# Narrow weight parts start up to 31 columns further into their tiles

## The chip, the cores and the metric

The kernel runs on one core of a Trainium2 chip. The metric is the device time of one execution in microseconds (us). TensorE multiplies, VectorE (DVE), ScalarE (ACT) and GpSimd (POOL) work on elements, and SyncE (SP) issues the transfers from HBM to the on-chip memory (SBUF, 128 partitions).

## The reference

Two transformer blocks, one after the other, on one sequence of 256 tokens with 1024 features, in fp32. The first block mixes gated MLP heads, forgetting attention and attention over a memory, and has a feed-forward layer of 4096. The second has two layers, each of them feed-forward, attention, feed-forward; its four feed-forwards are gated ones with a width of 2816:

```python
def swiglu(h, wg, wu, wd):
    return (jax.nn.silu(h @ wg) * (h @ wu)) @ wd
...
        x = x + 0.5 * swiglu(rmsnorm_2(x, ffn_norm1[i]), ffn1_wg[i], ffn1_wu[i], ffn1_wd[i])
```

Most of the work is the products of 256 tokens with weight matrices, 208.71 MB of which are read once.

## The kernel before

Activations lie transposed in SBUF: a tile holds 128 features (partitions) by 256 tokens. To keep fp32 accuracy with TensorE's fp32r format, each activation and each weight is split in two fp32r numbers, a high and a low part, and each product is made of three matmuls: high by high, low by high, high by low.

The class `Stream` brings in the weights. A list `order`, made from `seq` and `cuts`, names every transfer (a chunk of up to 2048 columns by 128 partitions) and how it is cut into parts of at most `PART = 1024` columns. There are 436 parts, numbered `i` in the order in which they are used. `split()` handles one part: ScalarE copies it from `raw` into the tile `wh{i % 6}` (line 103), which rounds it to fp32r, and one call later `low()` lets VectorE subtract that from `raw` and write the rest to `wl{i % 6}` (line 113). All of these tiles are 1024 columns wide whatever the part's width, and a part begins at column 0 of its tile. `get()` runs this up to `AHEAD = 4` parts ahead of the products. The order on each engine is the order of the program; nothing is reordered by a planner.

`mm_t` (lines 130 to 137) makes the products in which a slice of 128 columns of the weight tile is the stationary operand (loaded by an LDWEIGHTS that the trace calls PEld) and the activation tile of 256 columns is the moving one; each step over `k` has the three matmuls of lines 135, 136 and 137. In `mm_n` (lines 139 to 147) and `mm_y` (lines 149 to 161) the weights are the moving operand.

The parts of at most 768 columns: the down-projections `dn0` to `dn3` of the four gated feed-forwards (each of 16 transfers of 1408 columns, cut into 768 and 640, so 32 parts a stage and 128 in all), four parts of 768 of `w1v`, six parts of 512 or 768 of `uqv0` and `uqv1`, and one of 256 of `bin1`: 139 of 436. The parts of `w1f` have 780 columns. A down-projection loops over 8 output tiles `d`, each with four parts and 6 + 5 + 6 + 5 = 22 steps over `k`:

```python
            for d in range(KT):
                p = bank()
                for k0, n in ((0, DN_CUT), (DN_CUT, 11 - DN_CUT), (11, DN_CUT), (11 + DN_CUT, 11 - DN_CUT)):
                    mm_t(p[:, :T], ws.get(), 0, P, (ah[k0:], al[k0:]), range(n), k0 == 0, k0 == 11 + DN_CUT)
```

So a stage `dn` has 8 x 22 x 3 = 528 pairs of a weight load and a matmul. By the order of the parts, `dn0` has the parts 139 to 170, `dn1` 233 to 264, `dn2` 309 to 340 and `dn3` 404 to 435.

Of the kernel before, what the change touches and what calls it, by code (L numbers as in the profile page):

```python
# [24 lines left out]
PART = 1024  # L25
# [26 lines left out]
def block_kernel(ctx: ExitStack, tc: tile.TileContext, a: dict, out: bass.AP, upto: int = 99):  # L52
# [20 lines left out]
    class Stream:  # L73
# [20 lines left out]
        def split(self, eng=dve):  # L94
            i = self.ns
            while len(self.parts) <= i and self.nd < len(order):
                self.dma()
            if i >= len(self.parts):
                return False
            t, n, last = self.parts[i]  # L100
            h = wp.tile([P, PART], F32R, tag=f"wh{i % HL}", name=f"wh{i}")
            lo = wp.tile([P, PART], F32R, tag=f"wl{i % HL}", name=f"wl{i}")
            act.copy(h[:, :n], t)  # L103
            self.hl[i] = (h, lo)
            self.ns += 1
            self.low(eng)
            self.late = (lo[:, :n], t, h[:, :n], last)
            return True
# [495 lines left out]
    for nm, i0, i1 in seq:  # L604
        for i in range(i0, i1):
            src = [a[nm][i, 0], a[nm][i, 1]] if len(a[nm].shape) == 4 else [a[nm][i]]
            for ap in src:
                n = ap.shape[-1]
# [906 lines left out]
```

## Time and profile before

| | |
|---|---|
| median of 3 runs | 1241.44 us (1239.43 to 1244.65) |
| the profiled execution | 1249.46 us, its span 1247.7 us |
| TensorE, busy share of the span | 98% (9844 matmuls, 9844 weight loads) |
| VectorE, ScalarE, GpSimd, busy share | 67%, 53%, 14% |
| granted TensorE clock, mean | 0.991 |
| HBM read | 208.71 MB, 168 GB/s over the span |

A span runs from the first to the last instruction of the profiled execution. Matmuls overlap, so that a busy TensorE need not be at its peak: its pace is read from the distance between the starts of successive matmuls, here called a step. [...]

### The profile page before, as it was taken

Reading aid. Unit: us, or ns where it says so; the run is one execution under the profiler, and the core shown is the slowest. Engines: PE = TensorE matmul, PEld = TensorE weight load, DVE = VectorE, ACT = ScalarE, POOL = GpSimd, SP = SyncE. Lnnn points to the kernel's source line nnn. Section 1 sums busy time; section 2 is a strip of 40 time slices with the busy share of each in tenths; the row PEclk is TensorE's granted clock in tenths of the full one; section 3 lists DMA queues with packets and bytes.
Section 4 is the critical chain, followed back from the end, with each engine's and each line's share of the span. In section 5 each row is a group of like instructions: output and inputs, shape, how many; then the busy total and the mean of one; then the engine's idle time right before and its main releaser. Section 6 shows DMA issues by size and latency. Waiting matters only on the chain.

```text
span 1247.7 us, 23873 instructions
## 1 busy us (share of the span) xinstructions
PE 1221.4 (98%) x9844; PEld 1165.4 (93%) x9844; DVE 840.4 (67%) x1482; ACT 658.1 (53%) x1164; POOL 175.6 (14%) x169
## 2 busy tenths in 40 slices
PE   8999999999999999999999999999999989999998
PEld 7878899888899999988999999999999869999998
DVE  6786776754578666698666666666666797666553
ACT  5455765443554544577545444445454787545442
POOL 5422200300202001122100001100001462000000
PEclk9799999999999999999999999999999999999999
DMA  7524354655344545532555456545556422555463
GB/s 237 199 89 148 137 199 173 213 196 200 122 152 165 202 144 187 211 136 94 177 185 188 168 166 207 199 173 203 172 168 209 167 68 89 182 184 189 161 203 111
DMA packets 37262, 211.31 MB, mean 169 GB/s; under 512 B 4768, under 2 KB 8224, under 8 KB 18848
## 3 DMA queue, kind: packets, MB, share of 16 engines
q1 hardware_dynamic: 37152, 209.78, 48.6%
q8 instruction: 77, 1.26, 0.4%
q14 instruction: 33, 0.27, 0.1%
HBM read 208.71 MB, written 1.05 MB: 168 GB/s over the span
## 4 chain that ended last, share of the span: by engine, by line
PE 84%; DVE 10%; ACT 3%; issue 2%; DMA 1%; POOL 0%; SPq 0%; ACTq 0%; DVEq 0%
PE ps L135 23%; PE ps L137 23%; PE ps L136 23%; DVE wl L113 3%; PE ps L159 3%; PE ps L161 3%; PE ps L160 3%; PE ps L310 1%; PE ps L342 1%; PE ps L321 1%; DVE p L299 1%; DMA raw<-in_w1q 1%; PE ps L145 1%; PE ps L146 1%; ACT wh L103 1%
## 5 line engine op out<-in xcount | busy, mean ns | idle before, releaser
L113 DVE TENSOR_TENSOR wl<-raw,wh 128x1024 fp32r<-128x1024 f32 (+4 forms) x436 | 491.2, 1165 | 57.1 <-ACT wh L103 56.7
L135 PE MATMUL ps<-xh,wh 128*128 128x256 f32 (+1 forms) x1848 | 522.8, 283 | 2.2 <-DVE y L526 1.7
L137 PE MATMUL ps<-xh,wl 128*128 128x256 f32 (+1 forms) x1848 | 517.6, 280 | 2.5 <-DVE wl L113 2.5
L136 PE MATMUL ps<-xl,wh 128*128 128x256 f32 (+1 forms) x1848 | 518.5, 281 | 0.5 <-DVE xl L271 0.5
L103 ACT CAST wh<-raw 128x1024 fp32r<-128x1024 f32 (+4 forms) x436 | 400.2, 958 | 92.8 <-PE ps L160 37.8
L135 PEld LDWEIGHTS ps<-xh,wh 128*128 128x128 f32 (+1 forms) x1848 | 348.9, 189 | 5.0 <-ACT sq L208 2.1
L137 PEld LDWEIGHTS ps<-xh,wl 128*128 128x128 f32 (+1 forms) x1848 | 348.9, 189 | 3.0 <-DVE wl L113 2.9
L136 PEld LDWEIGHTS ps<-xl,wh 128*128 128x128 f32 (+1 forms) x1848 | 348.9, 189 | 0.9 <-DVE xl L271 0.7
L137 PE MATMUL ps<-ah,wl 128*128 128x256 f32 x704 | 195.7, 278 | 0.0
L136 PE MATMUL ps<-al,wh 128*128 128x256 f32 x704 | 195.4, 278 | 0.0
L135 PE MATMUL ps<-ah,wh 128*128 128x256 f32 x704 | 195.4, 278 | 0.0
L408 ACT ACTIVATE s<-t 128x256 f32<-128x256 f32 x88 | 36.9, 419 | 189.1 <-DVE t L406 189.1
L136 PEld LDWEIGHTS ps<-al,wh 128*128 128x128 f32 x704 | 132.3, 188 | 0.0
L137 PEld LDWEIGHTS ps<-ah,wl 128*128 128x128 f32 x704 | 132.2, 188 | 0.0
L135 PEld LDWEIGHTS ps<-ah,wh 128*128 128x128 f32 x704 | 131.9, 187 | 0.0
L209 POOL TENSOR_TENSOR acc<-acc,sq 128x256 f32<-128x256 f32 x49 | 55.2, 1127 | 516.7 <-ACT sq L208 516.2
L406 DVE TENSOR_TENSOR t<-ps,rb 128x256 f32<-128x256 f32 x88 | 37.2, 422 | 71.6 <-PE ps L137 65.0
L262 ACT ACTIVATE xh<-x,cols 128x256 fp32r<-128x256 f32 x56 | 28.5, 509 | 105.9 <-DVE x L454 94.6
L223 DVE TENSOR_TENSOR al<-f,ah 128x256 fp32r<-128x256 f32 (+1 forms) x104 | 48.8, 470 | 52.5 <-ACT ah L222 52.5
L222 ACT CAST ah<-f 128x256 fp32r<-128x256 f32 (+1 forms) x104 | 45.7, 440 | 56.6 <-DVE f L410 43.2
L410 DVE TENSOR_TENSOR f<-ps,s 128x256 f32<-128x256 f32 x88 | 37.4, 425 | 47.5 <-ACT s L408 47.5
L453 DVE SCALAR_TENSOR_TENSOR t<-ps,rb 128x256 f32<-128x256 f32 x32 | 13.6, 425 | 74.0 <-PE ps L137 74.0
(278 smaller groups left out, 1422.2 us busy)
## 6 DMA issues: line engine op xcount, KB each, us to landing
raw<-in_gu SPq DMA_DIRECT2D x88, 1024.0 KB, 4.8
raw<-in_dn SPq DMA_DIRECT2D x64, 704.0 KB, 4.4
raw<-in_ff SPq DMA_DIRECT2D x32, 1024.0 KB, 4.8
raw<-in_w_out SPq DMA_DIRECT2D x4, 1024.0 KB, 4.8
raw<-in_aq SPq DMA_DIRECT2D x4, 1024.0 KB, 5.0
raw<-in_a_out SPq DMA_DIRECT2D x4, 1024.0 KB, 5.7
raw<-in_b_out SPq DMA_DIRECT2D x4, 1024.0 KB, 5.0
raw<-in_w1q SPq DMA_DIRECT2D x6, 512.0 KB, 4.1
```

The lines of the kernel that those rows point to most:

```text
L103: act.copy(h[:, :n], t)
L113: eng.tensor_tensor(out=lo, in0=t, in1=h.bitcast(F32), op=ALU.subtract)
L135: pe.matmul(ps, lhsT=h[:, c:c + m], rhs=x[0][k], start=s0, stop=False)
L136: pe.matmul(ps, lhsT=h[:, c:c + m], rhs=x[1][k], start=False, stop=False)
L137: pe.matmul(ps, lhsT=lo[:, c:c + m], rhs=x[0][k], start=False, stop=s1)
L159: pe.matmul(ps, lhsT=x[0][k][:, ts], rhs=h[:, c:c + n], start=s0, stop=False)
L160: pe.matmul(ps, lhsT=x[1][k][:, ts], rhs=h[:, c:c + n], start=False, stop=False)
L161: pe.matmul(ps, lhsT=x[0][k][:, ts], rhs=lo[:, c:c + n], start=False, stop=s1)
L209: gp.tensor_tensor(out=acc, in0=acc, in1=sq, op=ALU.add)
L222: act.copy(h, src)
L223: dve.tensor_tensor(out=lo, in0=src, in1=h.bitcast(F32), op=ALU.subtract)
L410: dve.tensor_tensor(out=f, in0=u, in1=s, op=ALU.mult)
```

## The change

In `split()`, a part of at most 768 columns begins `o = i // 4 % 32` columns (of 4 bytes) into its `wh` and `wl` tiles, in place of column 0. `o` grows by one every four parts and starts again after 32; wider parts stay at column 0. The slices are handed on, so that the copy of line 103, the subtraction of line 113 and all matmuls of the part use the shifted places; `raw` and the activations stay where they are. The tiles, the transfers, the number and the order of instructions and the amount of work are the same. The largest place that is used is column 31 + 768 = 799 of 1024.

```diff
             h = wp.tile([P, PART], F32R, tag=f"wh{i % HL}", name=f"wh{i}")
             lo = wp.tile([P, PART], F32R, tag=f"wl{i % HL}", name=f"wl{i}")
+
+            o = i // 4 % 32 if n <= PART - 256 else 0
+            h, lo = h[:, o:], lo[:, o:]
             act.copy(h[:, :n], t)
             self.hl[i] = (h, lo)
             self.ns += 1
```

By the parts' numbers, `o` runs from 2 to 10 in `dn0`, from 26 to 31 and then 0 to 2 in `dn1`, from 13 to 21 in `dn2` and from 5 to 12 in `dn3`.

## Rows read from the trace of the kernel before

**Rows 1.** The page: the span, busy time by engine, the chain by engine.

```profile
span 1247.7 us, 23873 instructions
...
PE 1221.4 (98%) x9844; PEld 1165.4 (93%) x9844; DVE 840.4 (67%) x1482; ACT 658.1 (53%) x1164; POOL 175.6 (14%) x169
...
PE 84%; DVE 10%; ACT 3%; issue 2%; DMA 1%; POOL 0%; SPq 0%; ACTq 0%; DVEq 0%
```

**Rows 2.** The page's groups: busy us, mean ns | idle before, releaser.

```profile
L113 DVE TENSOR_TENSOR wl<-raw,wh 128x1024 fp32r<-128x1024 f32 (+4 forms) x436 | 491.2, 1165 | 57.1 <-ACT wh L103 56.7
...
L137 PE MATMUL ps<-xh,wl 128*128 128x256 f32 (+1 forms) x1848 | 517.6, 280 | 2.5 <-DVE wl L113 2.5
...
L137 PE MATMUL ps<-ah,wl 128*128 128x256 f32 x704 | 195.7, 278 | 0.0
```

**Rows 3.** Timeline: first and last matmul of dn0, dn1, dn2, dn3 (start, duration).

```profile
455.53 0.28 PE L135 MATMUL ps<-ah,wh 128*128 128x256 f32 x1
...
517.60 0.28 PE L137 MATMUL ps<-ah,wl 128*128 128x256 f32 x1
...
722.03 0.28 PE L135 MATMUL ps<-ah,wh 128*128 128x256 f32 x1
...
784.11 0.28 PE L137 MATMUL ps<-ah,wl 128*128 128x256 f32 x1
...
908.54 0.28 PE L135 MATMUL ps<-ah,wh 128*128 128x256 f32 x1
...
968.27 0.28 PE L137 MATMUL ps<-ah,wl 128*128 128x256 f32 x1
...
1183.85 0.28 PE L135 MATMUL ps<-ah,wh 128*128 128x256 f32 x1
...
1243.58 0.28 PE L137 MATMUL ps<-ah,wl 128*128 128x256 f32 x1
```

**Rows 4.** Timeline inside dn1: a matmul, the next weight load, its matmul.

```profile
739.00 0.28 PE L135 MATMUL ps<-ah,wh 128*128 128x256 f32 x1
739.00 0.19 PEld L136 LDWEIGHTS ps<-al,wh 128*128 128x128 f32 x1
739.11 0.28 PE L136 MATMUL ps<-al,wh 128*128 128x256 f32 x1
```

**Rows 5.** Timeline, four weight loads in a row between one-column matmuls.

```profile
22.15 0.52 PEld L229 LDWEIGHTS ps<-kon,acc 128*128 128x128 f32 x4
22.26 0.50 PE L229 MATMUL ps<-kon,acc 128*128 128x1 f32 x4
```

**Rows 6.** Timeline: first matmuls of four triplets of w1f at full clock.

```profile
11.14 0.34 PE L145 MATMUL ps<-wh,xh 128*128 128x390 f32 x1
...
11.67 0.34 PE L145 MATMUL ps<-wh,xh 128*128 128x390 f32 x1
...
12.21 0.34 PE L145 MATMUL ps<-wh,xh 128*128 128x390 f32 x1
...
12.74 0.34 PE L145 MATMUL ps<-wh,xh 128*128 128x390 f32 x1
```

**Rows 7.** Windows in dn1 and dn3: PE, PEld, DVE, ACT, POOL busy, PEclk, DMA.

```profile
730.00:780.00 50.00, 50.00 (x427) 50.00 (x426) 32.74 (x47) 24.22 (x40) 7.78 (x6) 1.00 0.57 193
...
1190.00:1240.00 50.00, 50.00 (x444) 50.00 (x443) 26.11 (x39) 18.58 (x24) 0.00 (x0) 1.00 0.55 181
```

**Rows 8.** Windows, DVE's line 113 alone in dn1.

```profile
730.00:780.00 50.00, 23.98 (x26) 1.00 0.57 193
```

**Rows 9.** Windows, ACT's line 103 alone in dn1.

```profile
730.00:780.00 50.00, 19.16 (x26) 1.00 0.57 193
```

## The prediction

> **What bounds the kernel now.** I read the page first, for the engine that sets the end. TensorE is busy for 98% of the span, and 84% of the chain that ended last are matmuls [rows 1]. The groups say whether TensorE waits for the weights: over the whole execution the matmuls of line 137 stood idle for 2.5 us until VectorE had written a `wl`, and in the down-projections, where the moving operand is `ah`, for 0.0 us [rows 2]. So the parts come in time, and what counts is the pace at which TensorE gets through pairs of a load and a matmul. Next the timeline, for that pace in the stages that the change touches. A stage `dn` has 528 pairs, so 527 steps from its first matmul to its last [rows 3]: `dn0` 62.07 us / 527 = 117.8 ns, `dn1` 62.08 / 527 = 117.8 ns, `dn2` and `dn3` 59.73 / 527 = 113.3 ns. The same program, then, has two paces, 4.4 ns apart; the clock is not the difference, as it is granted at 1.00 in a slow stage and in a fast one [rows 7]. The four stages' mean is 115.6 ns.
>
> What sets a step is seen one level deeper. In `dn1` the load for the next matmul starts when a matmul starts, at 739.00, and the next matmul starts 0.11 us later [rows 4]. The reader should compare this with the place where four loads follow each other with matmuls of a single column between them: the four take 0.52 us in all, one lasts 0.19 us as recorded [rows 4], so they start (0.52 - 0.19) / 3 = 0.11 us apart [rows 5]. With next to nothing to multiply, the step is as long as with 256 columns. The weight load therefore sets the pace, and the matmul hides under it. This is why the change has to be read as a change of loads: in `dn0` to `dn3` it is the stationary operand whose address moves.
>
> **The change part by part.** No instruction, byte, wait or transfer is added or removed, so queues, transfers and semaphores keep their order, SP's and POOL's included. What moves is the address of three kinds of operand.
>
> (a) Weight loads. 4 x 528 = 2112 loads of the down-projections read 128 columns from a start that is `o` columns further; `bin1`'s narrow part adds 8 x 3 = 24, which is 1% of that and goes with them. In a quarter of the parts `o` is a multiple of 4, so that the start moves by whole groups of 4 columns (16 bytes); in the others it moves by 1 to 3 columns more. No row of before shows a load that starts at such an odd place, so its cost is bounded. Below: the loads can gain what separates them from the step of loads with nothing to hide, 110 ns [rows 5]: (115.6 - 110) x 2112 = 11.8 us. Above: the slowest pace that a stage keeps is 4.4 ns over the fastest [rows 3]; if every load paid that much on top of its stage's pace, it would be 4.4 x 2112 = 9.3 us. The far end would be a load that no longer overlaps the previous one, at its recorded 0.19 us [rows 4]: (190 - 115.6) x 2112 = 157 us; nothing in the rows points there. I take 0 for the sum, because of the nearest row, which is (b)'s: an operand of TensorE that starts at an odd place of its tile runs as fast as one at the start.
>
> (b) Moving operands. In `w1v` and `uqv0/1` the weights stream past: 4 x 2 x 2 x 3 = 48 matmuls of `w1v`, 48 of the four query parts and 12 of the two value parts, 108 in all. Here the trace has a comparison. `w1f`'s parts of 780 columns hold two operands of 390, the second of which starts 390 x 4 = 1560 bytes into the tile, 8 bytes past a multiple of 16. At full clock the triplet from 11.14 (second half) takes 0.53 us, the one from 11.67 (first half) 0.54 us, the one from 12.21 (second half) 0.53 us [rows 6]. Odd start or not, the same within the 10 ns of the rows, so 3.3 ns a matmul: at most 108 x 3.3 = 0.4 us either way. I take 0.
>
> (c) ScalarE's copy and VectorE's subtraction write, and VectorE also reads, at the shifted place. No row shows either at such a place. At no change it costs nothing. What hides a longer one is TensorE's load-bound stage: in 50 us of `dn1` VectorE is busy 32.74 us and ScalarE 24.22 [rows 7], 23.98 us of it line 113 [rows 8] and 19.16 line 103 [rows 9]. VectorE becomes the bound only if line 113 takes (50 - 32.74) / 23.98 = 72% longer, ScalarE if line 103 takes 135% longer. Were line 113 twice as long, `dn1` would need 32.74 + 23.98 = 56.7 us for 50, 13% more; over the 243.6 us of the four stages 33 us at most, less in `dn3`, where VectorE has more room (26.11 of 50 [rows 7]). With that cover gone, TensorE would be late behind `wl`, the wait of line 137 that is 0.0 us in these stages now. One element a column passes either way, so I take no change in length and 0 in the sum.
>
> [...]
>
> The sum is 0: the profiled execution would stay at its 1249.46 us (1247.7 of span and 1.8 around it). That execution lies 8.0 us over the median of the three, 1241.44, and since nothing is added I forecast the median itself, 1241.4 us.
>
> **The rivals.** A measurement of this kernel can tell about 0.5%, 6.2 us, from no change. Spread over 2112 loads that is 2.9 ns a load: the four stages' mean step would have to leave 112.6 to 118.5 ns.
>
> Pace. The two paces of one program show that something in the timing of loads and matmuls settles for a stage and then holds. Another start address may make it settle otherwise. If `dn2` and `dn3` fall to the pace of the other two: + 4.4 x 1056 = +4.7 us, 1246.1. If `dn0` and `dn1` reach the faster one: -4.7 us, 1236.7. For it speaks that the slow stages exist; against it, that `dn1` and `dn2` run the same code on the same tiles and differ, so that the pace doesn't hang on an address alone. Both ends lie within 0.5%.
>
> Slower: loads pay for their odd start. [...] At 4.4 ns it is +9.3 us, 1250.7; it decides from 2.9 ns. For it: the load is the bottleneck, with nothing above it to hide a longer one. Against it: `w1f`. [...]
>
> Slower: VectorE's subtraction grows by over 72% and TensorE waits for `wl`. Up to +33 us, 1274. Against it: nothing in the trace suggests a stretch of that size.
>
> Faster: the moved start keeps loads and the streaming operand out of each other's way, and all loads come down to the 110 ns that they take with nothing beside them [rows 5]: -11.8 us, 1229.6. For it: 113 and 118 ns are both over 110, so something is lost. Against it: a shift that wanders over all places favours none.
>
> That the change doesn't do what it says can be excluded: the shift lies within the tile, and the slices go to every user.
>
> **How the numbers follow.** No effect on the pace: 0.40. Paces change between the two known ones, with a result within 0.5%: 0.15. Loads pay for a 33rd group, also within it: 0.10. Loads pay by more than 2.9 ns: 0.22. VectorE: 0.03. Faster: 0.10. So faster 0.10, same 0.40 + 0.15 + 0.10 = 0.65, slower 0.22 + 0.03 = 0.25. The range reaches down to the paces' better end, 1236.7, rounded to 1236, which leaves out most of the faster case (0.08), and up past the 1250.7 of the loads at 4.4 ns, to 1252, which leaves out the VectorE case and loads that pay still more (0.03 + 0.09). That is 0.20 outside.
>
> **What would show it.** Right: 527 steps in 59.7 to 62.1 us in each `dn` stage, whatever its `o`; lines 103 and 113 of 640 and 768 columns as long as before; no new wait of line 137 for `wl`. Wrong by the loads: steps over 118 ns in all four, and within a stage steps that differ between `d` whose parts have `o` a multiple of 4 and the others. Wrong by VectorE: line 113 at over 1.5 us and a wait behind it. Wrong by a gain: steps under 113 ns.

## The result, and the profile after

The changed kernel takes 1249.12 us (median of 3 runs, 1247.44 to 1250.05) against 1241.44 before: a ratio of 1.0063 with a 95% interval of 1.0044 to 1.0082, so 5.5 to 10.2 us more, 7.8 at the middle. The time lies inside the range that was forecast (1236 to 1252), but the forecast itself was no change (1241.4), and the change is a loss.

The page of the changed kernel, the lines that answer to [rows 1] and [rows 2]. Lines of `split()` and after it stand three further on: 138 to 140 are the old 135 to 137, 116 the old 113.

```profile
span 1247.3 us, 23873 instructions
...
PE 1218.5 (98%) x9844; PEld 1162.5 (93%) x9844; DVE 839.2 (67%) x1482; ACT 658.7 (53%) x1164; POOL 178.0 (14%) x169
...
L116 DVE TENSOR_TENSOR wl<-raw,wh 128x1024 fp32r<-128x1024 f32 (+4 forms) x436 | 490.7, 1164 | 57.3 <-ACT wh L106 56.9
...
L140 PE MATMUL ps<-ah,wl 128*128 128x256 f32 x704 | 197.6, 281 | 0.0
```

VectorE's subtraction takes 1164 ns on the mean against 1165 in [rows 2], and the matmuls of the down-projections still wait 0.0 us for it. So neither the elementwise work nor a wait has grown. The mean matmul with `ah` and `wl` is recorded with 281 ns in place of 278, and the stages say the rest. The timeline of the changed kernel, first and last matmul of `dn0` to `dn3`, as in [rows 3]:

```profile
450.15 0.28 PE L138 MATMUL ps<-ah,wh 128*128 128x256 f32 x1
...
512.64 0.28 PE L140 MATMUL ps<-ah,wl 128*128 128x256 f32 x1
...
715.96 0.28 PE L138 MATMUL ps<-ah,wh 128*128 128x256 f32 x1
...
778.01 0.28 PE L140 MATMUL ps<-ah,wl 128*128 128x256 f32 x1
...
902.21 0.28 PE L138 MATMUL ps<-ah,wh 128*128 128x256 f32 x1
...
964.56 0.28 PE L140 MATMUL ps<-ah,wl 128*128 128x256 f32 x1
...
1180.65 0.28 PE L138 MATMUL ps<-ah,wh 128*128 128x256 f32 x1
...
1243.20 0.28 PE L140 MATMUL ps<-ah,wl 128*128 128x256 f32 x1
```

That is 62.49, 62.05, 62.35 and 62.55 us, 249.44 in all, against 62.07, 62.08, 59.73 and 59.73, 243.61 in all, in [rows 3]: +5.8 us, nearly all of it in `dn2` and `dn3`. The mean step is 249.44 / (4 x 527) = 118.3 ns. Within a stage the steps are no longer alike: by the starts of its matmuls, the output tile `d` = 3 of `dn1`, most of whose parts are at column 29, has 114.5 ns, and `d` = 4 of `dn0`, mostly at column 7, has 120.5:

```profile
481.37 0.28 PE L138 MATMUL ps<-ah,wh 128*128 128x256 f32 x1
...
489.32 0.28 PE L138 MATMUL ps<-ah,wh 128*128 128x256 f32 x1
```

These are the first matmuls of `d` = 4 and 5 in `dn0`: 66 steps in 7.95 us, 120.5 ns.

Why are the two spans alike (1247.3 and 1247.7 us), then? The profiled execution of before ran 17 us of its start at half the clock (0.51 from 41 to 55 us and 0.50 from 96 to 99 us, where 1.00 is full speed). Windows over the part ahead of the feed-forward, of before and of the changed kernel (span, then PE, PEld, DVE, ACT, POOL busy, the granted clock, DMA share and rate):

```profile
0.00:142.00 142.00, 130.36 (x876) 112.08 (x876) 102.20 (x207) 78.40 (x156) 49.91 (x54) 0.94 0.49 170
```

```profile
0.00:137.00 137.00, 122.35 (x879) 103.94 (x880) 102.65 (x208) 78.56 (x157) 50.35 (x55) 1.00 0.51 177
```

About as many matmuls took 5 us longer at a mean clock of 0.94. Without them the execution of before would be some 5 us shorter, which goes with the medians.

### The profile page after: what moved, and what is told of

It is laid out like the page before. It is cut to its first block, busy times and chain, and to the rows that moved or that the text cites. A ratio compares the mean times of both kernels' runs of the same rounds, so it can differ in the third digit from the quotient of the medians.

```text
span 1247.3 us, 23873 instructions
## 1 busy us (share of the span) xinstructions
PE 1218.5 (98%) x9844; PEld 1162.5 (93%) x9844; DVE 839.2 (67%) x1482; ACT 658.7 (53%) x1164; POOL 178.0 (14%) x169
## 4 chain that ended last, share of the span: by engine, by line
PE 82%; DVE 11%; ACT 3%; issue 2%; DMA 1%; POOL 1%; SPq 0%; ACTq 0%; DVEq 0%
PE ps L138 23%; PE ps L139 22%; PE ps L140 22%; DVE wl L116 4%; PE ps L162 3%; PE ps L163 3%; PE ps L164 3%; PE ps L345 1%; PE ps L324 1%; PE ps L313 1%; DVE p L302 1%; DMA raw<-in_w1q 1%; ACT wh L106 1%; PE ps L148 0%; ACT ah L225 0%
## 5 line engine op out<-in xcount | busy, mean ns | idle before, releaser
L116 DVE TENSOR_TENSOR wl<-raw,wh 128x1024 fp32r<-128x1024 f32 (+4 forms) x436 | 490.7, 1164 | 57.3 <-ACT wh L106 56.9
```

What stands on the lines that cost most here:

```text
L116: eng.tensor_tensor(out=lo, in0=t, in1=h.bitcast(F32), op=ALU.subtract)
```

## The experiments

Theory A: in these stages the weight load sets the step, as the prediction reads [rows 4, 5], and its pace depends on the distance in memory between the place from which it reads the weights and the place from which the matmuls read their moving operand. Rivals: B, a load at an odd start (not a multiple of 4 columns) costs something; C, the pace is drawn when a stage begins, whatever the places; D, the place of the weights alone counts. A later addition, E: one distance may have two steady paces, and how a stage is entered decides which it keeps. No run was made on one more rival, that it is the matmul's own columns and not the load that set the step; what the traces show of it stands in the part on why the prediction was right and wrong.

Shifts of the weights below are made in `split()`; `DN0 = (139, 233, 309, 404)` are the first parts of the four stages. Stage times are from the first to the last start of their 528 matmuls, in one profiled execution of each kernel.

**The kernel before once more.** No edit.

> The kernel before, profiled once more. Theory A (the distance, within 32 columns, from the start of the moving operand to the start of the weight load sets the pace; with one and the same distance two paces can still settle): at column 0 each stage dn0 to dn3 comes out at 113.3 or at 117.8 ns a step and nowhere else, perhaps in another mix than 117.8, 117.8, 113.3, 113.3. Rival C (the pace is drawn when a stage begins and has nothing to do with places): the same two values here, but then also in the kernels with other shifts. Rival B (only an odd start costs): nothing to say on this one.

Timeline, first and last matmul of `dn0` and `dn1`:

```profile
450.30 0.28 PE L135 MATMUL ps<-ah,wh 128*128 128x256 f32 x1
...
512.37 0.28 PE L137 MATMUL ps<-ah,wl 128*128 128x256 f32 x1
...
715.71 0.28 PE L135 MATMUL ps<-ah,wh 128*128 128x256 f32 x1
...
775.44 0.28 PE L137 MATMUL ps<-ah,wl 128*128 128x256 f32 x1
```

`dn0` 62.07 us (117.8 ns), the other three 59.73 (113.3): 241.3 us in all. The same two values and another mix: `dn1` has changed sides from one execution to the next. Against this execution the changed kernel's stages cost 249.44 - 241.26 = 8.2 us more, against that of [rows 3] 5.8; the measured 7.8 lies between.

**A map of the places.**

```diff
+            o = next((8 * s + (i - i0) // 4 for s, i0 in enumerate(DN0) if i0 <= i < i0 + 32), 0)
+            h, lo = h[:, o:], lo[:, o:]
```

> Only the down-projections are shifted, and each output tile d has one shift of its own for its four parts: 8 x stage + d columns, so 0 to 7 in dn0, 8 to 15 in dn1, 16 to 23 in dn2, 24 to 31 in dn3. Theory A: each shift has the step that it had in the changed kernel, whatever the stage: about 120.8 ns at 7, 116.7 at 8, 120 at 15 and 16, 115.6 at 18, 113.3 at 29, within 0.5 ns. [...] Rival C (pace drawn at a stage's start): one step for all eight tiles of a stage.

The stages take 62.62, 62.51, 62.43 and 62.20 us, 118.5 ns a step on the mean. Timeline, first matmuls of neighbouring output tiles: `d` = 6 and 7 of `dn2` (shift 22), `d` = 5 and 6 of `dn3` (shift 29):

```profile
951.90 0.28 PE L138 MATMUL ps<-ah,wh 128*128 128x256 f32 x1
...
959.94 0.28 PE L138 MATMUL ps<-ah,wh 128*128 128x256 f32 x1
...
1223.04 0.28 PE L138 MATMUL ps<-ah,wh 128*128 128x256 f32 x1
...
1230.56 0.28 PE L138 MATMUL ps<-ah,wh 128*128 128x256 f32 x1
```

66 steps each: 8.04 us, 121.8 ns, and 7.51 us, 113.8 ns. The step changes from one output tile to the next inside a stage, which C, in its plain form, excludes. The whole map, worked out in this way (ns; the second line is from the next map, 32 columns further):

```
shift      0     1     2     3     4     5     6     7     8     9    10    11    12    13    14    15
map 1  117.8 118.4 119.9 119.9 116.7 117.3 119.9 120.7 116.7 119.9 117.8 119.9 117.3 119.8 117.7 120.1
+ 32   113.7 118.3 118.3 120.0 118.7 120.1 113.7 118.3 117.4 119.8 120.1 119.9 120.0 118.2 119.4 120.0
shift     16    17    18    19    20    21    22    23    24    25    26    27    28    29    30    31
map 1  120.0 118.3 115.6 116.9 118.4 119.9 121.8 116.9 118.4 119.8 119.2 117.8 117.9 113.8 117.9 119.5
+ 32   118.7 118.7 118.0 116.7 120.0 116.7 117.8 119.8 120.0 117.8 120.1 118.8 120.0 118.2 117.9 118.5
```

Shifts 12 and 16, multiples of 4, have 117.3 and 120.0, and the fastest is 29. The eight multiples of 4 of the first map have 117.9 on the mean, the other 24 have 118.7, and in the second map both have 118.5: an odd start (B) costs at most 0.8 ns in the one and nothing in the other. The values that the changed kernel gave are met where A named them (7, 8, 15, 16, 18, 29). At 11 and 12 they are not: there the parts at 11 had 117.8 in the changed kernel and those at 12 had 119.9. So a value of the table belongs to one place behind one neighbour, and need not be the only pace of that place.

**All down-projections at column 29.**

```diff
+            o = 29 if any(i0 <= i < i0 + 32 for i0 in DN0) else 0
+            h, lo = h[:, o:], lo[:, o:]
```

> All 128 parts of the down-projections start 29 columns into their tiles, an odd place, and all other parts at column 0. Theory A: 113.3 ns a step in all four stages, 59.7 us each, 238.9 us in all; that is 10.5 us less than in the changed kernel (249.4) and 0 to 4.7 us less than before, so a ratio to before of 0.996 to 1.000. [...] Rival C: a mix of 113.3 and 117.8 as before, ratio 1.000.

Timeline, first and last matmul of `dn0`:

```profile
450.74 0.28 PE L138 MATMUL ps<-ah,wh 128*128 128x256 f32 x1
...
510.50 0.28 PE L140 MATMUL ps<-ah,wl 128*128 128x256 f32 x1
```

59.76 us in each of the four stages, 113.4 ns, at an odd place. The ratio to before is 0.9988 (0.9971 to 1.0005), as A said: the shift as such costs nothing, and `dn0` has lost its slow pace. The ratio alone doesn't decide between A and C, as C's 1.000 lies in its interval.

**All down-projections at column 7.** As above, with 7.

> All 128 parts of the down-projections start at column 7, one of the slowest places of the first map (120.7 ns). Theory A: 527 x 120.7 ns = 63.6 us in each of four stages, 254.5 us in all, 13.2 us more than in the control (241.3) and 10.9 more than in the profile of before (243.6): ratio to before 1.009 to 1.011. Rival C (pace drawn at a stage's start): ratio 1.000. [...]

Timeline, first and last matmul of `dn0`:

```profile
450.51 0.28 PE L138 MATMUL ps<-ah,wh 128*128 128x256 f32 x1
...
514.13 0.28 PE L140 MATMUL ps<-ah,wl 128*128 128x256 f32 x1
```

63.62 us in each of the four, 120.7 ns as in the map, and a ratio of 1.0113 (1.0093 to 1.0132), where A said 1.009 to 1.011. The four stages are alike to the last digit although GpSimd works in the first three and rests in the fourth (here 6.37 us of 50 in `dn1` and 0.00 in `dn3`, with 30.54 and 24.84 of VectorE), so what these two do is not what sets the pace.

**The other narrow parts alone**: the change's shift in `w1v`, `uqv0`, `uqv1` and `bin1`, the down-projections at 0.

> The change in the eleven narrow parts that are not of the down-projections alone (w1v, uqv0, uqv1, bin1); the down-projections at column 0. Theory A: nothing to see, 108 matmuls with a moved moving operand and 24 loads; ratio to before 0.999 to 1.001. If the ratio is over 1.003, the down-projections are not the whole cause.

The ratio is 0.9998 (0.9984 to 1.0013). The down-projections are the whole of the loss. The trace does show the shift of the moving operand, though. Timeline, first and last matmul of the first of `w1v`'s four products of 12 matmuls, in before and in this run:

```profile
77.77 0.42 PE L145 MATMUL ps<-wh,xh 128*128 128x384 f32 x1
...
79.76 0.34 PE L147 MATMUL ps<-wl,xh 128*128 128x384 f32 x1
```

```profile
73.49 0.42 PE L148 MATMUL ps<-wh,xh 128*128 128x384 f32 x1
...
75.55 0.34 PE L150 MATMUL ps<-wl,xh 128*128 128x384 f32 x1
```

The four products take 1.99, 2.01, 2.01 and 2.02 us in before, 2.06, 2.04, 2.02 and 2.04 here, and 2.06, 2.04, 2.06 and 2.04 in the changed kernel: 0.1 to 0.2 us in all, too little for the time to show. But in the first product the step, once it is even, goes from 173 to 180 ns with the place, in a stage whose step is far over the 110 ns of a load [rows 5].

**Only the activations moved.** The weights stay at column 0.

```diff
+            fa.tile([P, pad], F32, name="pad")   # pad = 32, 24, 16, 8 in dn0 to dn3
             ah = [fa.tile([P, T], F32R, name=f"ah{j}") for j in range(22)]
```

> The weights stay at column 0 of their tiles everywhere. Only the activation tiles of the down-projections move, up by 32, 24, 16 and 8 columns in dn0 to dn3. Theory A (the distance between the two operands counts): each stage has the step that the weights have when they lie as much lower, that is by 64 columns' turn at the shifts 32, 40, 48 and 56 of the second map, the first tile of each of its stages. Rival D (the weights' own place counts): 113.3 or 117.8 ns in all four, as before.

Timeline, first and last matmul of `dn0` and `dn3`:

```profile
451.61 0.28 PE L136 MATMUL ps<-ah,wh 128*128 128x256 f32 x1
...
511.36 0.28 PE L138 MATMUL ps<-ah,wl 128*128 128x256 f32 x1
...
1179.49 0.28 PE L136 MATMUL ps<-ah,wh 128*128 128x256 f32 x1
...
1242.73 0.28 PE L138 MATMUL ps<-ah,wl 128*128 128x256 f32 x1
```

`dn0` 59.75 us, 113.4 ns (the map: 113.7 at shift 32); `dn3` 63.24 us, 120.0 ns (119.95 at 56); `dn2` 118.7 (118.7 at 48); `dn1` 118.7, where the map had 117.4 at 40. D falls: with the weights where they always were, the pace is that of another distance in three stages of four, and in none of the slow ones is it one of column 0's. That the distance alone counts, and not each of the two places, this doesn't show.

**The distance of shift 29 with both operands moved**: `pad` 0, 8, 16, 24 and shifts 61, 5, 13, 21.

> The activation tiles of the down-projections are moved as well, by 0, 8, 16 and 24 columns in dn0 to dn3, and the weights start at column 61, 5, 13 and 21 of their tiles, so that the distance between the two is in each stage that of shift 29, counted within 32 columns. Theory A (the distance counts): 113.3 ns a step, 59.7 us, in all four. Rival D (the place of the weights alone counts): as in the changed kernel for the same shifts, 117.3 ns for 5, 120 for 13, about 119.5 for 21, so 61.8, 63.2 and 63.0 us in dn1 to dn3; for 61 it has 113.3 if places repeat every 32 columns.

Timeline, first and last matmul of `dn1` and `dn2`:

```profile
717.54 0.28 PE L139 MATMUL ps<-ah,wh 128*128 128x256 f32 x1
...
777.30 0.28 PE L141 MATMUL ps<-ah,wl 128*128 128x256 f32 x1
...
901.52 0.28 PE L139 MATMUL ps<-ah,wh 128*128 128x256 f32 x1
...
963.80 0.28 PE L141 MATMUL ps<-ah,wl 128*128 128x256 f32 x1
```

59.76 us in `dn1` and 59.75 in `dn3`, as A said and against D, but 62.28 (118.2 ns) in `dn0` and `dn2`. Half a miss. One reason is that places don't repeat every 32 columns, which the next run was to show; but `dn1` and `dn2` have the same distance in the full sense, and differ.

**The map, 32 columns further.** `32 + 8 * s + ...` in place of `8 * s + ...`.

> The map again with 32 columns more: each output tile d of the down-projections has the shift 32 + 8 x stage + d. If places repeat every 32 columns, each step is that of the first map 32 columns below, within 0.5 ns: 116.7 at 36 and 40, 121.8 at 54, 113.3 to 113.8 at 61. If they repeat only every 64 or more, the two maps differ: after the run in which column 61 had 118.2 in dn0, this reading says 118.2 at 61. In both the mean over the 32 places is near 118.4, 62.4 us a stage.

The second lines of the table: 113.7 for 117.8 at 32, 118.2 for 113.8 at 61. Places don't repeat every 32 columns. The mean over 32 places is the same again, 249.9 / (4 x 527) = 118.5 ns.

**Two families of activations moved** to what was taken for the distance of shift 29, counted within 64 columns.

```diff
+    xh_ = res.tile([P, 43 + KT * T], F32R, name="xh")   # xl_: 59 + KT * T
+    xh = [xh_[:, 43 + k * T:43 + k * T + T] for k in range(KT)]
...
+            o = 77 if any(i0 <= i < i0 + 32 for i0 in DN0) else 0
```

> Theory A put to use. The split activations xh and xl, which the gate, up and first feed-forward products stream past, are moved so that the distance to the weights (at column 0) is the one that gave 113.3 ns in all four down-projections; the down-projections keep that distance by a shift of 77. Theory A: 113.3 ns in place of 116.7 to 117.8 in the 5,544 pairs with xh or xl, -18 us, and 59.7 us in each dn, -2 to -5 us: ratio to before 0.981 to 0.985. Rival D (the weights' own place counts): the products with xh and xl keep 116.7 to 117.8, and column 77 is some other place: ratio 0.998 to 1.01.

Timeline, first and last matmul of `dn1` and `dn2`:

```profile
714.77 0.28 PE L138 MATMUL ps<-ah,wh 128*128 128x256 f32 x1
...
778.01 0.28 PE L140 MATMUL ps<-ah,wl 128*128 128x256 f32 x1
...
903.44 0.28 PE L138 MATMUL ps<-ah,wh 128*128 128x256 f32 x1
...
963.17 0.28 PE L140 MATMUL ps<-ah,wl 128*128 128x256 f32 x1
```

A miss: 1.0082 (1.0062 to 1.0103). Three of the stages ran at 120.0 ns and `dn2`, with the same places, at 113.3; the products with `xh` and `xl` had 117.8. So theory A with one pace a distance is wrong. In the same run the matmuls of 512 columns in the feed-forward of the first block also changed. No shift touches their weights, but their stationary tiles are allocated behind `xh` and `xl`. A window inside that stage, of before and of this run:

```profile
235.00:305.00 70.00, 70.00 (x302) 56.40 (x301) 41.90 (x36) 27.41 (x30) 10.10 (x6) 1.00 0.60 210
```

```profile
235.00:305.00 70.00, 70.00 (x311) 57.96 (x310) 39.34 (x35) 29.46 (x31) 6.39 (x4) 1.00 0.61 217
```

By the starts of the matmuls that is a step of 226.7 ns here, and 233.3 to 233.4 in every other profile, twice the 110 ns of a load. That two paces belong to one place was in [rows 3] already (`dn1` and `dn2`); what chooses between them was the next question.

**Another way into a stage.** Everything at column 0 but the first part of each stage, its first 18 pairs.

```diff
+            o = {139: 29, 233: 7, 309: 29, 404: 7}.get(i, 0)
```

> All parts of the down-projections at column 0, but for the first part of each stage (18 pairs), which starts at column 29 in dn0 and dn2 and at column 7 in dn1 and dn3. Theory E (a distance has one or two steady paces, and the one that a stage keeps is decided by how it is entered): dn0, which has had 117.8 ns in both profiles at column 0, goes to 113.3 behind a fast first part; dn1 and dn3, which have had 113.3 in three of four, go to 117.8 behind a slow one. Theory A alone, with one pace for a distance: can't give both values at column 0 at all. Rival C' (the pace is drawn by chance): dn0 as likely 117.8.

Timeline, first and last matmul of `dn0` and `dn1`:

```profile
451.00 0.28 PE L138 MATMUL ps<-ah,wh 128*128 128x256 f32 x1
...
510.76 0.28 PE L140 MATMUL ps<-ah,wl 128*128 128x256 f32 x1
...
714.07 0.28 PE L138 MATMUL ps<-ah,wh 128*128 128x256 f32 x1
...
776.19 0.28 PE L140 MATMUL ps<-ah,wl 128*128 128x256 f32 x1
```

`dn0` 59.77, `dn1` 62.12, `dn2` 59.73, `dn3` 62.12 us: the 510 pairs at column 0 keep 113.3 ns behind a fast first part and 117.8 behind a slow one, four times out of four. How much that says depends on what the stages would have done without it, and the gate and up products ahead of them (`gu0` to `gu3`) tell: at places that only the run with two families moved and the version for use change, their last 120 matmuls have 116.7 or 117.8 ns a step. In the three profiles in which the down-projections are all at column 0 (before, the control, the other narrow parts alone), each of the twelve stages is slow behind 117.8 ns and fast behind 116.7. Windows inside `gu1` of before, ahead of a slow `dn1` (the control's, ahead of a fast one, has 774 matmuls and stands further down), and then inside `gu1` and `gu2` of this run:

```profile
610.00:700.00 90.00, 90.00 (x766) 90.00 (x765) 57.71 (x83) 44.53 (x66) 0.00 (x0) 1.00 0.52 180
```

```profile
620.00:710.00 90.00, 90.00 (x774) 90.00 (x773) 56.78 (x81) 43.12 (x65) 0.00 (x0) 1.00 0.52 182
805.00:895.00 90.00, 90.00 (x767) 90.00 (x766) 59.60 (x105) 43.44 (x65) 0.00 (x0) 1.00 0.52 180
```

In this run 116.7, 116.7, 117.8 and 116.7 ns stand ahead of `dn0` to `dn3`. So `dn1`, `dn2` and `dn3` left the pace that the stage ahead would have given them, and only `dn0` would have been fast without its first part. E holds at column 0, and chance (C') fits neither this nor the twelve stages. For other places the pace ahead is no rule: with two families moved all four stages had 117.8 ns ahead, and `dn2` alone was fast. The run at column 29 had 116.7 ahead of all four stages, and so doesn't show what that place does behind a slow one; the run at column 7 had both, and 120.7 in all four.

**Only `wl` at column 7**, `wh` at 0 (`lo = lo[:, 7:]` in the down-projections).

> In the down-projections only wl starts at column 7; wh stays at column 0. If each load pays by its own distance, a third of the loads have the 120.7 ns of column 7 and two thirds the 113.3 or 117.8 of column 0: 115.8 or 118.8 on the mean of a triplet, 61.0 or 62.6 us a stage. If the pace belongs to the cycle of three loads as a whole, any step from 113.3 to 122 can come out, the same within a stage.

Timeline, first and last matmul of `dn0`:

```profile
450.44 0.28 PE L138 MATMUL ps<-ah,wh 128*128 128x256 f32 x1
...
512.29 0.28 PE L140 MATMUL ps<-ah,wl 128*128 128x256 f32 x1
```

61.85 us in `dn0` and 61.83 in the other three, 117.3 ns, neither 115.8 nor 118.8: as was said ahead of the run, that speaks for a pace of the cycle of three loads as a whole, and against one of each load by its own place.

**A version for use.** All weights at column 0, and both families of activations moved to where the one run with moved activations had its fast stage.

```diff
+    res.tile([P, 40], F32, name="pad_x")
     xh = [res.tile([P, T], F32R, name=f"xh{k}") for k in range(KT)]
...
+            fa.tile([P, 56], F32, name="pad_a")
             ah = [fa.tile([P, T], F32R, name=f"ah{j}") for j in range(22)]
```

> All weights at column 0. The tiles xh and xl lie 40 columns further and the activation tiles of the down-projections 96 columns further than before, so that both stand to the weights as the activations of dn0 did in the run in which they alone were moved and dn0 had 113.3 ns. Theory A with one pace for this distance: 113.3 ns in the 5,544 pairs with xh or xl and in all four dn stages, ratio to before 0.981 to 0.986. Theory E (a second, slower pace of the same distance can settle): some stages at 113.3, others over 117, ratio 0.985 to 1.005.

Timeline, first and last matmul of `dn0`; then a window inside the gate and up products of `gu1`, in this kernel and in the control:

```profile
448.64 0.28 PE L135 MATMUL ps<-ah,wh 128*128 128x256 f32 x1
...
508.37 0.28 PE L137 MATMUL ps<-ah,wl 128*128 128x256 f32 x1
...
610.00:700.00 90.00, 90.00 (x797) 90.00 (x796) 59.18 (x86) 45.40 (x68) 0.00 (x0) 1.00 0.55 192
```

```profile
610.00:700.00 90.00, 90.00 (x774) 90.00 (x773) 57.91 (x82) 44.24 (x66) 0.00 (x0) 1.00 0.56 194
```

1226.43 us, ratio to before 0.9869 (0.9847 to 0.9891): faster than both kernels. All four down-projections have 59.73 us, and in the same 90 us `gu1` gets through 797 matmuls in place of 774, by their starts 113.4 ns for 116.7. The gain is a little less than A's 0.981 to 0.986, and lies in E's 0.985 to 1.005: the first products of the first block's feed-forward stayed at 117 to 118 ns. Two pads did it, no work was taken away.

## Why the prediction was right and wrong

- What bounds the stages was right in part. TensorE's step does set the time, with no wait in between: the 5.8 to 8.2 us that the four stages lost make up the kernel's 7.8, and a shift of 7 columns moved it by +1.1% and two pads by -1.3%, with the same work. That it is the load which sets the step is not shown. The steps with 384, 390 and 512 columns, 174 ns (`w1v`), 178 ns (`w1f`) and 233.3 ns (the first block's feed-forward), are 0.45 to 0.46 ns a column. An estimate from these for 256 columns is 116 to 117 ns, as near to the measured 113 to 122 as the 110 ns of loads with next to nothing to multiply [rows 5]. And where the clock of before was 0.51 (41 to 55 us), loads with matmuls of 6 columns started 213 ns apart, and pairs with 256 columns 213 ns as well. Places also moved the steps of 384 columns (173 to 180 ns) and of 512 (226.7 to 233.3), where the step is far over a load's 110 ns. Which of the two sets the step, no run separates.
- The step that failed is the one in (a): "I take 0 for the sum, because of the nearest row, which is (b)'s: an operand of TensorE that starts at an odd place of its tile runs as fast as one at the start." The row, `w1f` [rows 6], compares two places of a moving operand, at a step of (12.74 - 11.14) / 9 = 178 ns, and these two happen to be alike; `w1v`, a stage of the same kind, is not alike at other places. Two like places price neither the others nor a load's. In place of 0 the runs showed the mean over the places, 118.3 to 118.5 ns a step, against the 114.5 (241.3 us) to 115.6 ns of column 0: 2.8 to 3.9 ns more in the changed kernel, 5.8 to 8.2 us over the four stages. Of the signs of being right, 59.7 to 62.1 us in each stage, `dn1` alone kept it (62.05).
- The upper bound of (a) wasn't one. "The slowest pace that a stage keeps" was read from one place, column 0 with its two paces; single places go up to 121.8 ns. That its 9.3 us held, and with it the range, is luck: the change walks over all places and takes their mean.
- The rival of the loads that pay had the sign and the size (+9.3 us; measured 5.5 to 10.2) and the wrong mechanism. Its sign in the profile, steps that differ between multiples of 4 and the rest, was not there (117.9 and 118.7 ns in the first map, 118.5 and 118.5 in the second). The cost of an odd start is at most 0.8 ns a load in the first map and none in the second; column 29 ran at 113.4 ns with all down-projections there, and column 16 at 120.0 in the first map. The chance of 0.10 for loads that pay for "a 33rd group" rests on no row, and no run shows such a group; in its place the maps showed these 0.8 and 0 ns.
- The rival of the pace came nearest, at the wrong size: it let the stages move only between the two known paces. Its argument against itself, that `dn1` and `dn2` run the same code and differ, "so that the pace doesn't hang on an address alone", was true and was half of what the runs found (the places, and the way in).
- (b) was right for the time (0.9998), but its at most 3.3 ns a matmul was too small: the first product of `w1v` grew by 7. (c) and the rest were right: lines 106 and 116 took as long as before (ScalarE is busy for 658.7 us in place of 658.1, VectorE for 839.2 in place of 840.4), and no wait was added.

## What to carry to other kernels

In this kernel a stage in which TensorE alternates loads and matmuls of 256 columns ran at 113.3 and at 117.8 ns a step with the same instructions, both steady [rows 3]. Read the step between matmuls stage by stage, and where stages of one loop differ, try a pad of a few columns before the moving operand's tiles, which adds no work. Of two tries here one was worth 1.3% and one lost 0.8%, so each has to be measured. The shift of this change, which wanders over many places, got 118.3 ns a step, close to the 118.5 of either map, and lost because column 0 had had 114.5 to 115.6. And two places that come out alike in one row don't price the rest: where the same stage already shows two paces, as column 0 did, the nearest row is that stage, and not another one that happens to agree.

## What the runs showed of the hardware

In the down-projections the step of a load and matmul pair of 128 and 256 fp32r columns was 113.3 to 121.8 ns depending on the places of the two operands, with up to 6.4 ns between neighbouring columns (37 and 38); no order by multiples of 4 columns (117.9 ns on them and 118.7 beside them in the first map, 118.5 and 118.5 in the second), and no repetition after 32 (117.8 at 0 and 113.7 at 32; 113.8 at 29 and 118.2 at 61). Pairs with 384 and 512 columns moved too, from 173 to 180 and from 233.3 to 226.7 ns. One and the same place can hold two paces (113.3 and 117.8 at column 0; 113.3 and 120.0 in the run with two families moved), and in three stages 18 pairs at the head decided which one the next 510 kept (113.3 behind a part at column 29, 117.8 behind one at column 7). Left open is whether the load or the matmul's columns set the step, why the places matter, whether their distance alone does, after how many columns places repeat, and why what was taken for the distance of shift 29 held 113.4 ns in all four stages in one run, and 113.3 to 113.4 in half or a quarter of them in others; no run here tells that apart.
